# Emitting the convolutions of a hybrid decoder layer one attention half later, tied behind the score maxima

## The chip, the cores and the metric

The kernel runs on one core of one Trainium2 chip. The core has five engines that each work through their own list of instructions in order: PE (TensorE, matrix products), DVE (VectorE), ACT (ScalarE), POOL (GpSimd) and SP (SyncE, which here only issues transfers). They wait for one another through semaphores. The metric is the device time of one execution in microseconds (us); lower is better.

## The reference

One layer of a decoder that mixes sliding-window attention and a gated linear recurrence over T = 1024 tokens (plus 16 learned meta tokens in front, so 1040 rows), model width 1024, everything in float32. Cut to what matters:

```python
h = concat(meta, x)                       # 1040 x 1024
u = rmsnorm(h, g_pre_mix)
q, k, v, xr, yr = split(u @ w_in)         # widths 512, 128, 128, 512, 512
attn = sliding_window_attention(q, k, v, sinks)   # 8 heads, 2 kv heads, window 128
xr = causal_depthwise_conv(xr, conv_w, conv_b)    # 4 taps per channel
r, i = sigmoid(gate_r(xr)), sigmoid(gate_i(xr))   # block-diagonal products
a = exp(-8 * r * softplus(-lam))
hr = scan(h_t = a_t * h_(t-1) + sqrt(1 - a_t^2) * i_t * xr_t)
rec = gelu(yr) * hr
h = h + rmsnorm(concat(attn, rec) @ w_out, g_post_mix)
u = rmsnorm(h, g_pre_ffn)
h = h + rmsnorm(relu(u @ w_ff1)^2 @ w_ff2, g_post_ffn)
return h[16:]
```

A score is masked, its row maximum is taken together with the head's sink, and the exponentials are normalised by their sum plus that of the sink.

## The kernel before

**Precision.** A float32 product is made of three products of a narrower type. `split` (L94 to L100) takes a tile apart into a high part (a cast on ACT, L95, or on DVE, L97) and a low part (a subtraction on DVE, L98); `mm3` then issues three matmuls, high by high (L124), high by low (L125) and low by high (L126).

**Stages.** The normalised input `u` stays on chip in eight high and low pairs (`a` tiles). The projections come next: k, v, the first q and the first x chunk at the start, the rest during attention. Attention goes over four head pairs `j` and two halves of the tokens, eight steps in all. In each, `scores(j, half)` computes two score tiles (`bp` 0 and 1): matmuls into the bank `ps_s` (L525, L529), on DVE a fused masking and maximum (L545), on ACT the exponentials, on DVE a reciprocal (L555), on POOL the sum of the two window blocks (L559), on DVE the normalisation (L560). `attend` of the step before transposes the probabilities on PE (L571), splits them, masks them on POOL (L575), multiplies by the values (L585) and copies the result out (ACT L598, DVE L599).

**Fills.** After each `scores`, one further projection is issued to keep PE at work between the attention products: q1, x1, q2, x2, q3, x3, y0, y1 in the eight steps, y2 after the loop, and y3 after the gates. A fill loads its weight one step ahead (`load_cols`: a DMA into `raw`, then `split` into a `ws` pair), runs 24 matmuls a piece into `ps_acc` (L124 to L126, `ps_acc<-a,ws`) and evicts. For an x chunk the fill also runs the convolution `conv`: one `tensor_scalar` (L608) and three `scalar_tensor_tensor` (L613) on DVE, each over about 1040 columns. The y chunks are evicted by DVE copies (L640).

**What sets the order.** The program is written in one order, and a scheduler then orders the instructions of each engine by priority and dependencies. `deferred(FILL_LAG)` gives what is issued inside it a later priority by 1000, so that fills stand behind attention work that was issued later; steps in `Q_SLOTS` use 0. `behind(name, *instructions)` adds a dependency without a semaphore: the scheduler must place the instructions after the named one.

**After attention.** `gates(c)` for the four chunks (matmuls `ps_s`, `ps_pt`, `ps_o` `<-b,e`, each followed by a sigmoid on ACT, then `L715` on DVE), then for two pairs of chunks `decay` (an exponential and a tanh on ACT, L82 as all of its table functions) and `recur` (a square root on ACT, then on DVE L728, L729 and the scan L730). The output weights `wo[0]` to `wo[3]` are loaded and split: `wo[0]` on DVE alone (L97, then the low part L98 into `ws`), the others with their high part cast on ACT (`a<-raw`, `a<-d`). `rec_out` (gelu on ACT, L736 on DVE) gives the recurrent half of the mix. The output projection `out_mm` starts on the attention part: `ps_pt`, `ps_o`, `ps_acc`, `ps_s` `<-ws,b` and `<-a,b`. Then come the output norms (`out_norm`) and the feed-forward layer, which fill the rest of the time from about 350 us on.

Of the kernel before, what the change touches and what calls it, by code (L numbers as in the profile page):

```python
# [37 lines left out]
def hybrid_layer(  # L38
# [6 lines left out]
    nc = tc.nc  # L45
# [12 lines left out]
    def slot(tag, shape, dt=F32):  # L58
        uid[0] += 1
        return slab.tile(shape, dt, tag=tag, name=f"{tag}{uid[0]}", bufs=bufs[tag])  # L60

    def pair(tag, shape):
        return slot(tag, shape, F32R), slot(tag, shape, F32R)

    def bank(tag, shape=(P, 512)):
        uid[0] += 1
        return ps.tile(list(shape), F32, tag=tag, name=f"ps_{tag}{uid[0]}")

    def f32(ap):
        return ap.bitcast(F32)  # L70

    @contextmanager
    def deferred(n):
        tc.cur_priority += n
        yield
        tc.cur_priority -= n
# [4 lines left out]
    def lut(*args, **kwargs):  # L81
        ins = nc.scalar.activation(*args, **kwargs).ins  # L82
        if last_lut[0] is not None:
            tc.add_manual_dep(
                ins, last_lut[0],
                mybir.DependencyInfo(
                    mybir.DependencyClass.NoSync, mybir.DependencyReason.DATA
                ),
                reason="lut",
            )  # L90
        last_lut[0] = ins.name

    def split(hi, lo, src, eng=None):
        if eng is None:  # L94
            nc.scalar.copy(hi, src)  # L95
        else:
            eng.tensor_copy(hi, src)  # L97
        low = nc.vector.tensor_tensor(lo, src, f32(hi), op=ALU.subtract).ins  # L98
        mark[0] = low.name
        return low  # L100
# [4 lines left out]
    def behind(name, *inss):  # L105
        for ins in inss:
            tc.add_manual_dep(
                ins, name,
                mybir.DependencyInfo(
                    mybir.DependencyClass.NoSync, mybir.DependencyReason.DATA  # L110
                ),
                reason="order",
            )
# [60 lines left out]
    last_pow = [None]  # L174


    def load_cols(cols, tag="ws"):
        raw = slot("raw", [P, KC, P])
        o = 0
        for c0, n in cols:  # L180
            w, lo = c0
            nc.sync.dma_start(
                raw[:, :, o : o + n],
                w[:, lo : lo + n].rearrange("(k p) c -> p k c", p=P),
            )
            o += n
        hi, lo_ = pair(tag, [P, KC, P])
        split(hi, lo_, raw)
        return hi, lo_

    def w_q(j):
        return load_cols([((w_in, Q_COL + P * j), P)])

    def w_x_chunk(c):
        return load_cols([((w_in, X_COL + P * c), P)])

    def w_y_chunk(c):
        return load_cols([((w_in, Y_COL + P * c), P)])
# [19 lines left out]
    def project(w, pieces, sink):  # L218
        wh, wl = w
        for t0, n in pieces:  # L220
            acc = bank("acc")
            for kc in range(KC):
                uh, ul = u[kc]
                mm3(
                    acc[:, :n], (wh[:, kc, :], wl[:, kc, :]),
                    (uh[:, t0 : t0 + n], ul[:, t0 : t0 + n]),
                    kc == 0, kc == KC - 1,
                )
            sink(acc[:, :n], t0, n)
# [160 lines left out]
    def new_x(tag="d"):  # L390
        xr = slot(tag, [P, TT])

        def sink_x(acc, t0, n):
            nc.scalar.copy(xr[:, t0 : t0 + n], acc)

        return xr, sink_x
# [106 lines left out]
    def at_pair(cp):  # L503
        for half in range(2):
            at[half][cp] = pair("b", [P, 2, 512])


    def scores(j, half, q):

        g, pairs = j // 2, []  # L510
        for bp in range(2):
            sn = slot("c", [P, 4, 257])
            negm = small.tile([P, 4], F32, name="negm", tag="negm")
            den = small.tile([P, 4], F32, name="den", tag="den")
            rden = small.tile([P, 4], F32, name="rden", tag="rden")
            nc.vector.tensor_copy(
                sn.rearrange("p (h i) k -> p h i k", h=2)[:, :, :, 256],
                nsink[:, 2 * j : 2 * j + 2].to_broadcast([P, 2, 2]),
            )
            for h in range(2):  # L520
                sp_ = bank("s", (P, 2, 256))

                def qk(dst, b, hi, lo):
                    c = slice(b * P, (b + 1) * P)
                    nc.tensor.matmul(  # L525
                        dst, q[h][:, c], hi, start=True, stop=False,
                        skip_group_check=True,
                    )
                    nc.tensor.matmul(  # L529
                        dst, q[h][:, c], lo, start=False, stop=True,  # L530
                        skip_group_check=True,
                    )

                for i in range(2):
                    b = 4 * half + 2 * bp + i
                    if b == 0:
                        qk(sp_[:, i, 0:P], b, km[:, g, 0, :], km[:, g, 1, :])
                        qk(sp_[:, i, P:256], b, khh[g][:, 0:P], kl[g][:, 0:P])
                    else:
                        c = slice((b - 1) * P, (b + 1) * P)  # L540
                        qk(sp_[:, i, :], b, khh[g][:, c], kl[g][:, c])
                for i in range(2):
                    b = 4 * half + 2 * bp + i
                    k = 2 * h + i
                    nc.vector.tensor_tensor_reduce(  # L545
                        out=sn[:, k, 0:256], in0=sp_[:, i, :],
                        in1=mask1 if b == 0 else mask, scale=-1.0,
                        scalar=nsink[:, 2 * j + h : 2 * j + h + 1],
                        op0=ALU.add, op1=ALU.min, accum_out=negm[:, k : k + 1],
                    )  # L550
                    lut(
                        sn[:, k, :], sn[:, k, :], AF.Exp, scale=-1.0,
                        bias=negm[:, k : k + 1], accum_out=den[:, k : k + 1],
                    )
            nc.vector.reciprocal(rden, den)  # L555


            one = sn[:, :, 0:P]
            nc.gpsimd.tensor_tensor(one, one, sn[:, :, P:256], op=ALU.add)  # L559
            nc.vector.tensor_tensor(one, one, rden.to_broadcast([P, 4, P]), op=ALU.mult)  # L560
            pairs.append(sn)
        return pairs
# [40 lines left out]

    xc = [None] * NLRU

    def conv(c, xr, tag="d"):
        y = slot(tag, [P, TT])
        nc.vector.tensor_scalar(  # L608
            y, xr, prm[:, c, 3:4], prm[:, c, 4:5], op0=ALU.mult, op1=ALU.add
        )  # L610
        for k in (2, 1, 0):
            s = 3 - k
            nc.vector.scalar_tensor_tensor(  # L613
                y[:, s:], xr[:, : TT - s], prm[:, c, k : k + 1], y[:, s:],
                op0=ALU.mult, op1=ALU.add,
            )
        xc[c] = y

    ys = [None] * NLRU

    def fill_q(j):
# [3 lines left out]
            qs[j] = q  # L625
        return run

    def fill_x(c):
        def run(w):
            xr, sink = new_x()  # L630
            project(w, ALL, sink)
            conv(c, xr, "b" if c == 3 else "d")
        return run

    def fill_y(c):
# [9 lines left out]

    qs = [q0] + [None] * 3
    conv(0, xr0)
    fills = []
    for kind, j in (("q", 1), ("x", 1), ("q", 2), ("x", 2), ("q", 3), ("x", 3)):
        if kind == "q":  # L650
            fills.append((lambda j=j: w_q(j), fill_q(j)))
        else:
            fills.append((lambda j=j: w_x_chunk(j), fill_x(j)))
# [4 lines left out]
    def next_fill():  # L658
        i = len(loaded) - 1
        if i + 1 < len(fills):  # L660
            loaded.append(fills[i + 1][0]())
        else:
            loaded.append(None)
        fills[i][1](loaded[i])
# [3 lines left out]
    for j in range(NPAIR):  # L668
        for half in range(2):
            if j % 2 == 0 and half == 0:  # L670
                at_pair(j // 2)
            sn = scores(j, half, qs[j])
            with deferred(0 if (j, half) in Q_SLOTS else FILL_LAG):
                next_fill()
            if prev is not None:
                attend(*prev)
            prev = (j, half, sn)
    with deferred(FILL_LAG):
        next_fill()
    attend(*prev)  # L680
# [678 lines left out]
```

## Time and profile before

| what | value |
|---|---|
| median of 3 runs | 963.28 us (963.26 to 963.48) |
| the profiled execution's own time | 963.19 us |
| its span, first to last instruction | 960.8 us |
| mean granted clock of PE | 0.998 |
| attention (first scores L525 at 60.4 us) with fills, up to the gates | 60 to 200 us |
| gates, recurrence and the first output products, about | 200 to 270 us |

A row of the timeline has the start and the length in us, the engine, the line, the operation and `out<-in` by the names of the tiles; square brackets give the idle time before it and what ended it. A row of a chain or a group has the same names. `x2` stands for two instructions that are shown as one. A row of the waits says which engine waited for which, in us in all, how often, and the longest.

### The profile page before, as it was taken

The page shows a single profiled execution, that of the slowest core. Times are in us where ns is not written, and L with a number is a line of the kernel's source. Part 1 is how long each engine was busy: PE and PEld are TensorE (multiplying, and loading weights), DVE is VectorE, ACT ScalarE, POOL GpSimd, SP SyncE. Part 2 cuts the span into 40 slices and gives each one's busy share as a digit, 9 for nine tenths or more (in the row PEclk, how much of TensorE's full clock was granted, in tenths as well). Part 3 has the DMA queues.
Part 4 walks back from the last instruction along what each step waited for, and adds up shares of the span by engine and source line. Part 5 has one row for each costly group of instructions (what it writes and reads, how often), then busy time and mean ns, then how long its engine had stood idle before and what let it go on. Part 6 is the DMA issues. An engine that isn't in the chain of part 4 may idle for free.

```text
span 960.8 us, 12386 instructions
## 1 busy us (share of the span) xinstructions
PE 941.4 (98%) x4654; PEld 789.1 (82%) x4654; DVE 669.6 (70%) x945; ACT 501.1 (52%) x822; POOL 156.7 (16%) x202
## 2 busy tenths in 40 slices
PE   6999999999999999999999999999999999999997
PEld 6999998888788877888888888788888888888886
DVE  5579989756955796664655465568557776779884
ACT  7556676469634663443555556554433343435441
POOL 4015656600021100000111001100111100003020
PEclk9999999999999999999999999999999999999999
DMA  8111101111235457676546557623667765556422
GB/s 293 46 48 42 39 7 45 41 58 67 87 132 175 150 180 224 192 263 197 197 161 216 163 193 252 213 95 120 171 171 192 194 225 194 180 196 155 110 88 87
DMA packets 85626, 140.74 MB, mean 146 GB/s; under 512 B 5784, under 2 KB 48936, under 8 KB 85568
## 3 DMA queue, kind: packets, MB, share of 16 engines
q1 hardware_dynamic: 75104, 108.51, 34.5%
q0 software_dynamic: 9600, 29.36, 11.7%
q10 hardware_dynamic: 864, 2.10, 0.6%
q8 instruction: 36, 0.59, 0.3%
q14 instruction: 22, 0.18, 0.1%
HBM read 115.70 MB, written 23.07 MB: 144 GB/s over the span
## 4 chain that ended last, share of the span: by engine, by line
PE 88%; issue 5%; ACT 3%; DVE 2%; DMA 1%; POOL 1%; DVEq 0%; SPq 0%; POOLq 0%; ACTq 0%
PE ps_acc L124 11%; PE ps_acc L125 10%; PE ps_acc L126 10%; PE ps_s L126 6%; PE ps_s L125 6%; PE ps_s L124 6%; PE ps_pt L124 6%; PE ps_pt L125 6%; PE ps_pt L126 6%; PE ps_o L124 5%; PE ps_o L126 5%; PE ps_o L125 5%; PE ps_o L585 1%; ACT c L82 1%; PE ps_s L525 1%
## 5 line engine op out<-in xcount | busy, mean ns | idle before, releaser
L95 ACT CAST ws<-raw 128x1024 fp32r<-128x1024 f32 (+1 forms) x70 | 71.8, 1025 | 122.6 <-PE ps_o L125 45.1
L98 DVE TENSOR_TENSOR ws<-raw,ws 128x1024 fp32r<-128x1024 f32 (+1 forms) x71 | 86.3, 1215 | 47.9 <-ACT ws L95 47.8
L124 PE MATMUL ps_acc<-a,ws 128*128 128x256 f32 (+2 forms) x256 | 85.2, 333 | 0.0
L125 PE MATMUL ps_acc<-a,ws 128*128 128x256 f32 (+2 forms) x256 | 84.8, 331 | 0.0
L126 PE MATMUL ps_acc<-a,ws 128*128 128x256 f32 (+2 forms) x256 | 84.8, 332 | 0.0
L98 DVE TENSOR_TENSOR b<-b,b 128x1024 fp32r<-128x1024 f32 (+2 forms) x48 | 57.6, 1200 | 27.0 <-PE ps_o L125 17.4
L95 ACT CAST ws<-e 128x1024 fp32r<-128x1024 f32 x42 | 43.9, 1045 | 60.3 <-PE ps_o L125 26.7
L98 DVE TENSOR_TENSOR ws<-e,ws 128x1024 fp32r<-128x1024 f32 x42 | 51.3, 1222 | 23.0 <-ACT ws L95 23.0
L95 ACT CAST b<-b 128x1024 fp32r<-128x1024 f32 (+2 forms) x48 | 49.5, 1030 | 34.2 <-DVE b L862 33.4
L575 POOL TENSOR_SCALAR_AFFINE_SELECT c<-c 128x512 fp32r<-128x512 f32 x64 | 55.7, 893 | 27.3 <-ACT c L95 15.4
L169 POOL TENSOR_TENSOR rs<-ms,half_pow 128x1 f32<-128x1 f32 (+1 forms) x29 | 21.0, 730 | 211.0 <-DVE ms L165 209.6
L126 PEld LDWEIGHTS ps_acc<-a,ws 128*128 128x128 f32 x256 | 48.2, 188 | 4.9
L124 PEld LDWEIGHTS ps_acc<-a,ws 128*128 128x128 f32 x256 | 48.2, 188 | 4.2
L125 PEld LDWEIGHTS ps_acc<-a,ws 128*128 128x128 f32 x256 | 48.1, 188 | 4.2
L124 PE MATMUL ps_acc<-ws,b 128*128 128x512 f32 (+1 forms) x120 | 46.3, 386 | 0.0
L125 PE MATMUL ps_acc<-ws,b 128*128 128x512 f32 (+1 forms) x120 | 46.0, 384 | 0.0
L126 PE MATMUL ps_acc<-ws,b 128*128 128x512 f32 (+1 forms) x120 | 46.0, 384 | 0.0
L125 PE MATMUL ps_pt<-ws,b 128*128 128x512 f32 x112 | 44.2, 395 | 0.6 <-DVE ws L98 0.6
L126 PE MATMUL ps_pt<-ws,b 128*128 128x512 f32 x112 | 43.9, 392 | 0.0
L124 PE MATMUL ps_pt<-ws,b 128*128 128x512 f32 x112 | 43.9, 394 | 0.0
L124 PE MATMUL ps_s<-ws,b 128*128 128x512 f32 x110 | 43.3, 395 | 0.0
L126 PE MATMUL ps_s<-ws,b 128*128 128x512 f32 x110 | 43.2, 393 | 0.0
(393 smaller groups left out, 2713.4 us busy)
## 6 DMA issues: line engine op xcount, KB each, us to landing
raw<-in_w_ff_dram SPq DMA_DIRECT2D x58, 512.0 KB, 4.3
e<-in_w_ff_dram SPq DMA_DIRECT2D x42, 512.0 KB, 3.9
raw<-in_w_in_dram SPq DMA_DIRECT2D x12, 512.0 KB, 4.9
d<-in_w_ff_dram SPq DMA_DIRECT2D x12, 512.0 KB, 3.8
s_dram<-d POOLq DMA_DIRECT2D x12, 512.0 KB, 3.9
e<-in_w_ff_dram POOLq DMA_DIRECT2D x10, 512.0 KB, 5.4
raw<-in_w_ff_dram POOLq DMA_DIRECT2D x10, 512.0 KB, 5.6
c<-in_x_dram SPq DMA_DIRECT2D x8, 512.0 KB, 8.1
```

What stands on the lines that cost most here:

```text
L82: ins = nc.scalar.activation(*args, **kwargs).ins
L95: nc.scalar.copy(hi, src)
L98: low = nc.vector.tensor_tensor(lo, src, f32(hi), op=ALU.subtract).ins
L124: nc.tensor.matmul(dst, lh, rh, start=start, stop=False, skip_group_check=True)
L125: nc.tensor.matmul(dst, lh, rl, start=False, stop=False, skip_group_check=True)
L126: last_mm[0] = nc.tensor.matmul(dst, ll, rh, start=False, stop=stop, skip_group_check=True).ins.name
L169: last_pow[0] = nc.gpsimd.tensor_tensor(rs[:n], ms[:n], half_pow[:n], op=ALU.pow).ins.name
L525: nc.tensor.matmul(dst, q[h][:, c], hi, start=True, stop=False, skip_group_check=True,)
L575: nc.gpsimd.affine_select(out=m[:, :, side, :], in_=f32(m)[:, :, 1, :], pattern=[[0, 4], [-sign, P]], compare_op=op, fill=0.0, base=0, cha ...
L585: nc.tensor.matmul(po[:, :, oc : oc + n], v, m[:, :, pc : pc + n], start=first and k == 0, stop=last and k == 1, skip_group_check=True,)
```

## The change

Two things move, and no operation is added or taken away. The low part of each weight that `load_cols` fetches is tied behind a maximum, the last one (`h` = 1, `i` = 1) of the first score tile (`bp` = 0) of the latest `scores` issued by then. And a fill of an x chunk no longer emits its convolution: it puts it on the list `waiting`, and the loop emits it after the `scores` of the next step, outside the deferred priority, with its four instructions tied behind that step's maximum in the same way. The convolution of chunk 0, before the loop, stays as it was.

```diff
+    first_max = [None]
+
     def load_cols(cols, tag="ws"):
...
         hi, lo_ = pair(tag, [P, KC, P])
-        split(hi, lo_, raw)
+        low = split(hi, lo_, raw)
+        if first_max[0]:
+            behind(first_max[0], low)
         return hi, lo_
...
-                    nc.vector.tensor_tensor_reduce(
+                    top = nc.vector.tensor_tensor_reduce(
                         out=sn[:, k, 0:256], in0=sp_[:, i, :],
...
-                    )
+                    ).ins
+                    if bp == 0:
+                        first_max[0] = top.name
...
-    def conv(c, xr, tag="d"):
+    def conv(c, xr, tag="d", after=None):
         y = slot(tag, [P, TT])
-        nc.vector.tensor_scalar(
+        taps = [nc.vector.tensor_scalar(
...
+        if after:
+            behind(after, *taps)
...
+    waiting = []
+
     def fill_x(c):
         def run(w):
             xr, sink = new_x()
             project(w, ALL, sink)
-            conv(c, xr, "b" if c == 3 else "d")
+            waiting.append((c, xr, "b" if c == 3 else "d"))
         return run
...
             sn = scores(j, half, qs[j])
+            while waiting:
+                conv(*waiting.pop(), first_max[0])
             with deferred(0 if (j, half) in Q_SLOTS else FILL_LAG):
                 next_fill()
...
+    while waiting:
+        conv(*waiting.pop())
     with deferred(FILL_LAG):
         next_fill()
```

More of the change, by code (lines that the diff above doesn't have):

```diff
@@ L604, in hybrid_layer @@
     xc = [None] * NLRU
-    def conv(c, xr, tag="d"):
+    def conv(c, xr, tag="d", after=None):
         y = slot(tag, [P, TT])
-        nc.vector.tensor_scalar(
+        taps = [nc.vector.tensor_scalar(
             y, xr, prm[:, c, 3:4], prm[:, c, 4:5], op0=ALU.mult, op1=ALU.add
-        )
+        ).ins]
         for k in (2, 1, 0):
             s = 3 - k
-            nc.vector.scalar_tensor_tensor(
+            taps.append(nc.vector.scalar_tensor_tensor(
                 y[:, s:], xr[:, : TT - s], prm[:, c, k : k + 1], y[:, s:],
                 op0=ALU.mult, op1=ALU.add,
-            )
+            ).ins)
         xc[c] = y
+        if after:
+            behind(after, *taps)
     ys = [None] * NLRU
```

## The prediction

> **What bounds the kernel now.** I read the page's share of busy time first, then what PE waited for, then busy time by stretches of the stage that the change touches, then the chain of waits there.
>
> ```profile
> span 960.8 us, 12386 instructions
> ...
> PE 941.4 (98%) x4654; PEld 789.1 (82%) x4654; DVE 669.6 (70%) x945; ACT 501.1 (52%) x822; POOL 156.7 (16%) x202
> ...
> PEclk9999999999999999999999999999999999999999
> ...
> PE 88%; issue 5%; ACT 3%; DVE 2%; DMA 1%; POOL 1%; DVEq 0%; SPq 0%; POOLq 0%; ACTq 0%
> ```
>
> PE is busy for 941.4 of 960.8 us, at full clock, and carries 88% of the chain that ended last. Anything on another engine counts only where PE runs dry. So the question is which waits of PE the change makes, lengthens or removes. PE's own waits (columns: total, times, longest) are few:
>
> ```profile
> PE ps_s L126 <- DVE ws L98: 1.9, 2, 1.1
> PE ps_s L525 <- DVE negm L545: 1.7, 2, 1.3
> ...
> PE ps_acc L124 <- ACT a L1057: 0.7, 1, 0.7
> PE ps_pt L124 <- ACT a L95: 0.6, 1, 0.6
> PE ps_pt L125 <- DVE ws L98: 0.6, 1, 0.6
> ```
>
> The windows show in which stretch they lie (span 960.8, columns: length, then each engine's busy time, then PE clock):
>
> ```profile
> 150.00:160.00 10.00, 8.27 (x62) 7.68 (x62) 9.84 (x20) 5.99 (x16) 5.88 (x4) 1.00 0.26 76
> 160.00:200.00 40.00, 40.00 (x232) 34.93 (x231) 34.09 (x62) 22.72 (x50) 18.85 (x20) 1.00 0.16 47
> 200.00:230.00 30.00, 30.00 (x154) 26.52 (x154) 10.11 (x11) 23.16 (x36) 0.00 (x0) 1.00 0.11 36
> 230.00:250.00 20.00, 18.85 (x81) 14.72 (x80) 20.00 (x19) 19.93 (x25) 0.00 (x0) 1.00 0.23 80
> 250.00:350.00 100.00, 100.00 (x467) 82.05 (x467) 72.04 (x105) 50.80 (x111) 12.76 (x25) 1.00 0.48 158
> 940.00:960.80 20.80, 14.41 (x80) 12.29 (x78) 11.32 (x23) 4.37 (x14) 0.00 (x0) 0.89 0.26 101
> ```
>
> PE idles for 1.73 us in 150 to 160 us (10.00 less 8.27) and for 1.15 us in 230 to 250. In 160 to 230 and 250 to 350 it never idles. The remaining idle time lies at the ends or later than 350 us. The waits for `L1057` and `ps_s L126` with `ws` are outside the stretch that changes.
>
> The gap at 155 us by the chain of waits:
>
> ```profile
> 152.98 1.20 DVE d L613
> 154.18 1.57 DVE ws L98
> 155.75 0.40 DVE c L545
> ...
> 156.19 1.10 ACT c L82 x4
> ...
> 158.68 0.35 PE ps_s L525
> ```
>
> A convolution tap (`L613`) and then the low part of a fetched weight (`L98`, `ws`) stand on DVE ahead of the maxima (`L545`), so ACT's exponentials and PE's next scores (`L525`) come late. It looks like just what the change is meant for.
>
> **The change part by part.** It adds and removes no instruction: each engine has as many as before. The ties carry no semaphore, so no engine waits for anything new; they only limit the order that the scheduler may write down. What they do is therefore read from the order of the built program's instructions on each engine, set beside that of before.
>
> Ties. Nine low parts (all fetched weights but the first, which is loaded before any maximum exists) and twelve taps (three convolutions of four) are tied. Up to about 162 us of before, every engine's order is the same instruction by instruction, both convolutions there and their low parts included: the tie is to the maxima of the first score tile of that half, and these operations stood behind those already. The gap above, between the maxima of the *next* tile, keeps its cause. Cost and gain: 0.
>
> The third convolution and the low part beside it. Here order does change (half 0 and 1 of the last head pair, some 165 to 195 us): DVE gets the last score tile's normalisation (`L560`) ahead of `ws` low and the first tap instead of behind, the taps are interleaved otherwise, and PE's transposes (`L571`) and value products (`L585`) shift by a few places among the projection's matmuls.
>
> ```profile
> 174.06 1.12 DVE L608 TENSOR_SCALAR b<-d,prm 128x1040 f32<-128x1040 f32 x1
> ...
> 182.02 1.35 DVE L613 SCALAR_TENSOR_TENSOR b<-d,prm,b 128x1037 f32<-128x1037 f32 x1
> ```
>
> ```profile
> 203.44 1.08 ACT L95 CAST b<-b 128x1040 fp32r<-128x1040 f32 x1
> ```
>
> The convolution ended at 183.4 us and its result `b` is first read by ACT's cast at 203.44. Some 20 us cover it, so its move costs 0 (if the cover were gone, it would cost the delay itself). PE has no idle time from 160 to 200, and following each engine in the new order with the durations of before, I find every input of its shifted products ready 2 us or more ahead. So 0 here as well, but this is the least certain 0.
>
> What does matter is the consequence. With the last `L585` some 2.5 us earlier, eight projection matmuls (`ps_acc<-a,ws`) that stood ahead of the recurrence's gates now stand behind their start, and six of them behind all gates.
>
> ```profile
> 199.58 0.40 PE L126 MATMUL ps_acc<-a,ws 128*128 128x512 f32 x1
> 199.81 0.32 PE L124 MATMUL ps_s<-b,e 128*128 128x348 f32 x1
> ...
> 231.25 0.62 PE L124 MATMUL ps_pt<-ws,b 128*128 128x512 f32 x2
> ...
> 233.60 0.50 PE L125 MATMUL ps_pt<-ws,b 128*128 128x512 f32 x1 [0.56 <-DVE ws L98]
> ...
> 245.54 0.72 PE L124 MATMUL ps_pt<-a,b 128*128 128x512 f32 x2 [0.59 <-ACT a L95]
> ```
>
> One such matmul takes 0.23 us (199.58 to 199.81). The first gate product thus starts about 1.85 us earlier (8 x 0.23) and the last ends 6 x 0.23 = 1.38 us earlier; PE's total work is the same, so it reaches the output projection (231.25) when it did. Every ACT step that follows the gates (sigmoids, exponentials, square roots) moves by 1.38 us. The first square root, 226.56, becomes 225.18.
>
> DVE follows, and its order after that square root is another. Before:
>
> ```profile
> 227.66 1.24 DVE L728 SCALAR_TENSOR_TENSOR c<-b,c 128x1040 f32<-128x1040 f32 x1 [4.75 <-ACT c L82]
> 228.82 0.69 DVE L97 CAST ws<-raw 128x1024 fp32r<-128x1024 f32 x1
> 229.42 0.68 DVE L640 COPY d<-ps_acc 128x512 f32<-128x512 f32 x1
> 230.02 1.23 DVE L728 SCALAR_TENSOR_TENSOR c<-b,c 128x1040 f32<-128x1040 f32 x1
> 231.17 1.24 DVE L729 TENSOR_TENSOR c<-c,c 128x1040 f32<-128x1040 f32 x1
> 232.32 1.22 DVE L98 TENSOR_TENSOR ws<-raw,ws 128x1024 fp32r<-128x1024 f32 x1
> 233.46 1.22 DVE L98 TENSOR_TENSOR a<-raw,a 128x1024 fp32r<-128x1024 f32 x1
> 234.59 1.24 DVE L729 TENSOR_TENSOR c<-c,c 128x1040 f32<-128x1040 f32 x1
> 235.75 2.32 DVE L730 TENSOR_TENSOR_SCAN c<-b,c 128x1040 f32<-128x1040 f32 x1
> 237.98 0.67 DVE L640 COPY d<-ps_acc 128x512 f32<-128x512 f32 x1
> ```
>
> From the first `L728` at 227.66 to the low part of `wo[0]` (`ws`, 232.32) it was 4.66 us, with `L728`, `L97`, `L640`, `L728`, `L729` between. In the new order these stand there: `L728`, `L728`, `L729`, `L97`, `L640`, `L729`, `L730`, and only then `ws` low. By start-to-start steps: 1.15 + 1.15 + 1.15 + 0.60 + 0.60 + 1.15 (all from the rows above) + 2.23 (`L730`, 235.75 to 237.98) = 8.03 us. The start is 227.66 - 1.38 = 226.28, so `ws` low starts at 234.31 instead of 232.32: 1.99 us later. PE waits for exactly this (the row 233.60, 0.56 us, `<-DVE ws L98`). It has nothing else in its order to do, so its stop becomes 2.55 us: **+1.99**. `wo[0]`'s high part (`L97`) ends near 230.4, PE needs it at 231.25: 0. The queue behind `ws` low on DVE (`wo[1]` low, the second scan, evictions `L640`) is awaited by PE some 3 us later than it comes: 0.
>
> The other stop is at 245.54: 0.59 us for ACT's cast of `wo[3]`.
>
> ```profile
> 226.56 2.04 ACT L82 ACTIVATE c<-c 128x1040 f32<-128x1040 f32 x2
> ...
> 244.46 1.03 ACT L95 CAST a<-raw 128x1024 fp32r<-128x1024 f32 x1
> ```
>
> That cast is bound by the gelus and square roots ahead, so it comes 1.38 us earlier, at 243.08, and is done at 244.1. PE, late by 1.99 and taking it 10.16 us after its resumption in the new order, arrives at 235.59 + 10.16 = 245.75. The stop goes: **-0.59**. Next late would be `wo[3]`'s low part, near 247.5 against 251.5: covered.
>
> After 270 us PE's order is that of before. On SP, two loads of x for the output norms (`L805`) swap places with a neighbour; on POOL one mask (`L575`) does. ACT and DVE differ up to about 345 us (one early weight cast ahead of a norm). PE had no idle time in 250 to 350, and I find slack of 5 us or more: 0.
>
> Sum: +1.99 - 0.59 = +1.40 on the profiled execution. That took 963.19 us (960.8 span and 2.4 around it), 0.1 below the median of 963.28. Span 962.2, time **964.6 us**, +0.15%.
>
> Bounds: if the scan does not delay `ws` low and only the second stop goes, -0.6 gives 962.6. If the gates come no earlier, `ws` low starts 1.99 + 1.38 = 3.37 later and the second stop, which PE then meets 3.4 us later, goes too: +2.8; with 0.6 of new delay among the shifted `L585`, +3.4. I take the middle because the order of the instructions, which both ends contradict in one step each, gives it.
>
> [...] Nearest row: PE's clock is 1.00 over the stretch with the 1.73 us gap, while over the last 20.8 us, where PE is busy for only 14.41, it is 0.89. [...]
>
> **The rivals.**
> (1) Slower, 966.0: the gates do not come earlier. Place: ACT between the gates and the first square root. If a table load or a late input of the gates holds ACT so that the first `L728` starts at 227.66 as before, PE's stop is 3.93 us: +3.37 - 0.59 = +2.8. It passes the 0.2% from a first `L728` later than 226.9. For it: ACT ran these steps back to back, so a small loss early is kept. Against it: PE had no idle time from 160 to 230 us, so the gates' inputs were there before PE came to them.
> (2) Slower by the clock, 968.3: as (1), and the stop lowers PE's clock. Price by the row of the last stretch: 0.11 x 20.8 = 2.3 us on top. For it, only that row; against it, that PE did not idle that long in any row between. [...]
> (3) The change does nothing that counts, 963.2: something holds PE elsewhere ahead of `ws` low, or DVE runs ahead enough that its order there doesn't show. For it: nine tenths of the order is the same. Against it: DVE has no idle time at all in 230 to 250 (20.00 of 20.00), so work put ahead must delay.
> (4) Faster, 960.9: the 1.73 us gap closes as the change is meant to do it, and the 0.59 stop goes, with `ws` low not delayed: -2.3. Against it: the order on DVE around that gap is the same as before.
>
> **How the numbers follow.** About 0.2% (1.9 us, so 961.4 to 965.2) is what a measurement of this kernel can tell from no change. Forecast (964.6, give or take 0.5 for durations): 0.48, within. (1), and any unseen stop in the shifted products of like size: 0.27, slower. (2): 0.05, slower. (3): 0.12, within. (4): 0.05, faster; other gains: 0.03, which would need idle time that PE hardly has. Durations may carry a part of the forecast across 965.2; I move 0.03 for that. Faster 0.08, same 0.57, slower 0.35. The range reaches from 962.5, just under the lower bound, to 967.0 (the upper bound of +3.4 with some for durations); (2), (4) and half of what lies beside are left out, near 0.15.
>
> **What would show it.** Right: in the changed kernel's waits, PE `ps_pt L125 <- DVE ws L98` at about 2.5 us near 235.6; no wait of `ps_pt L124 <- ACT a L95`; the scan (`L730`) ahead of `ws` low on DVE; the first gate product near 198; the 1.7 us for `negm L545` unchanged. Wrong: a new wait of PE between 160 and 200 us, a stop near 233 that isn't longer, a window with a clock under 1.00 around 235, or any difference beyond 350 us.

## The result, and the profile after

Over eleven executions of each, the changed kernel takes 965.93 us in the median (963.45 to 969.48) against 962.91 us (961.27 to 963.48) before: the ratio is 1.0033, with a 95% interval of 1.0022 to 1.0045. It is slower, by some 3 us. The time lies inside the stated range (962.5 to 967.0) and above the single value (964.6).

The waits of PE in the changed kernel (columns: total, times, longest; later lines of the code have moved, so that L525 of before is L529, L545 is L549):

```profile
PE ps_pt L125 <- DVE ws L98: 2.5, 1, 2.5
PE ps_s L529 <- DVE negm L549: 1.7, 2, 1.3
...
PE ps_acc L124 <- ACT a L1071: 0.7, 1, 0.7
PE ps_s L126 <- DVE ws L98: 0.7, 1, 0.7
```

The stop for `ws L98` at `ps_pt` has grown from 0.6 to 2.5 us, the wait for ACT's cast (`ps_pt L124 <- ACT a L95`) is gone, and the 1.7 us for the maxima are as they were. The same windows as before:

```profile
150.00:160.00 10.00, 8.28 (x62) 7.69 (x62) 9.84 (x20) 6.02 (x16) 5.85 (x4) 1.00 0.25 74
160.00:200.00 40.00, 40.00 (x233) 34.94 (x232) 33.76 (x62) 22.77 (x50) 18.00 (x20) 1.00 0.16 47
200.00:230.00 30.00, 30.00 (x152) 26.28 (x151) 11.06 (x12) 24.42 (x37) 0.00 (x0) 1.00 0.10 36
230.00:250.00 20.00, 17.47 (x70) 13.81 (x69) 20.00 (x21) 19.36 (x24) 0.00 (x0) 0.91 0.31 97
250.00:350.00 100.00, 100.00 (x467) 82.03 (x466) 69.08 (x99) 48.64 (x107) 12.80 (x25) 1.00 0.43 144
600.00:625.00 25.00, 24.34 (x106) 19.47 (x105) 13.54 (x16) 13.85 (x14) 2.53 (x4) 1.00 0.66 216
```

From 230 to 250 us PE is busy for 17.47 us instead of 18.85, and PE's clock, 1.00 in every other row here, is 0.91. In 600 to 625 us the execution profiled before had PE idle for 1.86 us and this one for 0.66; a further execution of the same changed kernel had 1.70, so this is not of the change. It hides 1.2 us of the loss in the spans of the two profiles, 960.8 and 963.0 us.

The order of DVE that the prediction read out of the program is there (L742 is the former L728, L743 the former L729, L744 the scan):

```profile
226.51 2.39 DVE L742 SCALAR_TENSOR_TENSOR c<-b,c 128x1040 f32<-128x1040 f32 x2 [3.14 <-ACT c L82]
228.82 1.24 DVE L743 TENSOR_TENSOR c<-c,c 128x1040 f32<-128x1040 f32 x1
229.97 0.69 DVE L97 CAST ws<-raw 128x1024 fp32r<-128x1024 f32 x1
...
231.17 1.24 DVE L743 TENSOR_TENSOR c<-c,c 128x1040 f32<-128x1040 f32 x1
232.32 2.32 DVE L744 TENSOR_TENSOR_SCAN c<-b,c 128x1040 f32<-128x1040 f32 x1
234.56 1.20 DVE L98 TENSOR_TENSOR ws<-raw,ws 128x1024 fp32r<-128x1024 f32 x1
```

The scan stands ahead of the low part of `wo[0]`, which starts at 234.56 (the prediction had 234.31). And this is what PE makes of it:

```profile
232.89 0.40 PE L124 MATMUL ps_acc<-ws,b 128*128 128x512 f32 x1
235.81 0.80 PE L125 MATMUL ps_pt<-ws,b 128*128 128x512 f32 x1 [2.53 <-DVE ws L98]
236.41 0.63 PE L126 MATMUL ps_pt<-ws,b 128*128 128x512 f32 x1
236.83 0.63 PE L124 MATMUL ps_pt<-a,b 128*128 128x512 f32 x1
...
238.97 0.53 PE L126 MATMUL ps_o<-ws,b 128*128 128x512 f32 x1
239.33 0.39 PE L124 MATMUL ps_o<-a,b 128*128 128x512 f32 x1
239.56 0.39 PE L125 MATMUL ps_o<-ws,b 128*128 128x512 f32 x1
```

The row at 235.81 has the stop, 2.53 us. What follows was not in the sum: the matmuls start 0.43 us apart (236.41 to 236.83) until 239.33, and 0.23 us apart from there on. In a finer cut of the same stretch (columns as above):

```profile
234.50:235.00 0.50, 0.00 (x0) 0.00 (x0) 0.50 (x2) 0.50 (x1) 0.00 (x0) 1.00 0.00 0
...
235.50:236.00 0.50, 0.19 (x1) 0.19 (x2) 0.50 (x2) 0.50 (x1) 0.00 (x0) 0.84 0.00 0
236.00:236.50 0.50, 0.50 (x2) 0.40 (x3) 0.50 (x1) 0.50 (x2) 0.00 (x0) 0.50 0.00 0
...
238.50:239.00 0.50, 0.50 (x3) 0.36 (x2) 0.50 (x1) 0.50 (x1) 0.00 (x0) 0.50 0.97 123
239.00:239.50 0.50, 0.50 (x3) 0.46 (x2) 0.50 (x2) 0.50 (x1) 0.00 (x0) 0.74 0.61 205
239.50:240.00 0.50, 0.50 (x3) 0.40 (x3) 0.50 (x2) 0.49 (x2) 0.00 (x0) 1.00 0.83 328
```

By the means of the first and the last row under 1.00, PE ran at half clock from 235.84 to 239.26, which is 3.4 us. Eight matmuls take 3.52 us (235.81 to 239.33) where eight at the old spacing take 1.85: **1.67 us** on top of the stop.

### The profile page after: what moved, and what is told of

Same layout as the page of the kernel before. It is cut to its first block, busy times and chain, and to the rows that moved or that the text cites. A ratio compares the mean times of both kernels' runs of the same rounds, so it can differ in the third digit from the quotient of the medians.

```text
span 963.0 us, 12388 instructions
## 1 busy us (share of the span) xinstructions
PE 943.4 (98%) x4654; PEld 790.6 (82%) x4654; DVE 669.6 (70%) x945; ACT 501.2 (52%) x822; POOL 156.0 (16%) x202
## 4 chain that ended last, share of the span: by engine, by line
PE 89%; issue 4%; DVE 3%; ACT 2%; DMA 1%; POOL 1%; DVEq 0%; SPq 0%; POOLq 0%
PE ps_acc L124 11%; PE ps_acc L125 11%; PE ps_acc L126 11%; PE ps_s L126 6%; PE ps_pt L125 6%; PE ps_s L125 6%; PE ps_s L124 6%; PE ps_pt L126 6%; PE ps_pt L124 6%; PE ps_o L125 5%; PE ps_o L126 5%; PE ps_o L124 5%; PE ps_o L591 1%; ACT c L82 1%; PE ps_o L850 1%
## 5 line engine op out<-in xcount | busy, mean ns | idle before, releaser
L95 ACT CAST ws<-raw 128x1024 fp32r<-128x1024 f32 (+1 forms) x70 | 71.8, 1025 | 127.6 <-PE ps_o L125 45.3
L98 DVE TENSOR_TENSOR ws<-raw,ws 128x1024 fp32r<-128x1024 f32 (+1 forms) x71 | 86.1, 1213 | 42.3 <-ACT ws L95 42.3
L124 PE MATMUL ps_acc<-a,ws 128*128 128x256 f32 (+2 forms) x256 | 85.3, 333 | 0.0
L95 ACT CAST ws<-e 128x1024 fp32r<-128x1024 f32 x42 | 43.9, 1045 | 61.4 <-PE ps_o L125 26.8
L98 DVE TENSOR_TENSOR b<-b,b 128x1024 fp32r<-128x1024 f32 (+2 forms) x48 | 57.6, 1201 | 25.9 <-PE ps_o L125 17.4
L98 DVE TENSOR_TENSOR ws<-e,ws 128x1024 fp32r<-128x1024 f32 x42 | 51.4, 1223 | 22.8 <-ACT ws L95 22.8
L95 ACT CAST b<-b 128x1024 fp32r<-128x1024 f32 (+2 forms) x48 | 49.5, 1030 | 33.0 <-DVE b L876 32.2
L124 PEld LDWEIGHTS ps_acc<-a,ws 128*128 128x128 f32 x256 | 48.2, 188 | 4.2
L124 PE MATMUL ps_acc<-ws,b 128*128 128x512 f32 (+1 forms) x120 | 46.2, 385 | 0.0
L124 PE MATMUL ps_pt<-ws,b 128*128 128x512 f32 x112 | 43.9, 394 | 0.0
L124 PE MATMUL ps_s<-ws,b 128*128 128x512 f32 x110 | 43.3, 395 | 0.0
```

Of the source, the lines that this page charges most:

```text
L124: nc.tensor.matmul(dst, lh, rh, start=start, stop=False, skip_group_check=True)
```

## The experiments

Theory A: two terms make the loss, the longer stop for the low part of `wo[0]` and the half clock that the stop brings about. Rival B: the stop alone counts, and the low clock is a coincidence of one execution. Rival C: the loss comes from the attention work that the change shifts, and the stop is a side effect.

The order of the built programs answers one question without a run. With the tie of the fetched low parts alone, every engine's order is that of before; with the moved convolutions alone, it is that of the whole change. The low parts' tie does nothing.

**The changed kernel again** (no edit).

> The changed kernel once more, as the reference point for the runs beside it. Theory A (two terms: the scan now stands ahead of the low part of wo[0] on DVE, which makes PE stop for about 2.5 us, and a stop of that length halves PE's clock for some 3.4 us, which costs another 1.6 us): a stop of 2.5 us of PE for DVE ws L98 near 236, PE clock 0.50 from there to about 239.5, time 965 to 966. Rival B (the stop alone is the loss, the low clock seen once is a coincidence of that execution): the stop of 2.5 us again, but the clock at 1.00 behind it.

965.13 us, ratio 1.0030 [1.0017, 1.0044]. The stop was 2.5 us and the clock was 0.50 from 234.33 to 237.74: in a second profile of the program half clock again, and for 3.4 us again. B's coincidence is unlikely. But this time the low clock began 0.3 us *before* PE resumed (at 234.67), while in the first profile it began right behind the resumption (235.84, behind 235.81).

**The low part ahead of the scan.** On DVE two neighbours are swapped; nothing else differs in any engine's order.

```diff
+    load_wo(0, "raw")
+    low0 = split_wo(0, "ws", nc.vector)
     for cs in ((0, 1), (2, 3)):
...
-        nc.vector.tensor_tensor_scan(r, av[c], gi, 0.0, ...)
+        scans[c] = nc.vector.tensor_tensor_scan(r, av[c], gi, 0.0, ...).ins
+        if c == 0:
+            behind(low0.name, scans[c])
...
-    load_wo(0, "raw")
...
-    split_wo(0, "ws", nc.vector)
```

> The changed kernel with one swap: the low part of wo[0] stands directly ahead of the first scan on DVE instead of directly behind it; PE, ACT and the rest stand as in the changed kernel. Theory A: the low part starts 2.24 us earlier, PE's stop shrinks from 2.53 to about 0.3 us, the clock stays at 1.00, and PE, now some 3.9 us earlier, meets ACT's cast of wo[3] again with a stop of about 1 us: 2.9 us less than the changed kernel, within 0.2% of the kernel before. Rival B: stop of 0.3 but only about 1.2 us gained. Rival C (the loss comes from the shifted attention work, not from this stop): time stays at 965 to 966.

962.28 us, ratio 0.9995 [0.9983, 1.0007], on the same chip as the run before it. Waits of PE:

```profile
PE ps_pt L124 <- ACT a L95: 0.5, 1, 0.5
...
PE ps_pt L125 <- DVE ws L98: 0.3, 1, 0.3
```

The window from 230 to 250 us has PE busy for 19.20 us and a clock of 1.00. One swap takes back 2.85 us, as much as A's expectation said (2.9), while the attention part stays that of the changed kernel. C, in the form that all the loss comes from there, is out. By the stops alone (2.53 to 0.31, and 0.49 at the cast) B would give 1.73 us; with the clock A gives 3.4. The intervals leave about 1.7 us either way on the measured 2.85, so the times lean to A without deciding; what decides is the clock of 1.00 in the profile.

**A stop in between.** The first scan is cut in two and the low part of `wo[0]` stands between the pieces; x is 780 in one kernel and 520 in the other.

```diff
-        nc.vector.tensor_tensor_scan(r, av[c], gi, 0.0, ...)
+        first = nc.vector.tensor_tensor_scan(r[:, :x], av[c][:, :x], gi[:, :x], 0.0, ...).ins
+        load_wo(0, "raw")
+        low = split_wo(0, "ws", nc.vector)
+        behind(first.name, low)
+        rest = nc.vector.tensor_tensor_scan(r[:, x:], av[c][:, x:], gi[:, x:], r[:, x-1:x], ...).ins
+        behind(low.name, rest)
```

> The changed kernel with the first scan cut in two at column 780 of 1040; the low part of wo[0] stands between the pieces. PE's stop should be 0.3 + 780/1040 of 2.24 = 2.0 us. Theory A in its loose form (a stop of 2 us already counts as idle): clock 0.50 for some 3.4 us behind it, time 0.5 us under the changed kernel. Theory A in a strict form (it takes more than 2 us): clock 1.00, time 2.2 us under the changed kernel.

> As the run before with the cut at column 520: a stop of 0.3 + 1.12 = 1.4 us, little more than the 1.26 us of the gap at 158 us behind which the clock stayed at 1.00. Theory A: no lower clock, time 2.5 us or so under the changed kernel, and a stop of 0.3 us or less at the cast of wo[3]. If the clock falls here too, the gap at 158 us was spared for another reason than its length.

Cut at 780: 965.31 us, ratio 1.0031 [1.0019, 1.0044]. Cut at 520: 964.16 us, 1.0016 [1.0006, 1.0026]. PE with the cut at 780:

```profile
233.15 0.40 PE L124 MATMUL ps_acc<-ws,b 128*128 128x512 f32 x1
235.54 0.50 PE L125 MATMUL ps_pt<-ws,b 128*128 128x512 f32 x1 [1.99 <-DVE ws L98]
...
236.80 0.39 PE L124 MATMUL ps_pt<-a,b 128*128 128x512 f32 x1
237.03 0.58 PE L125 MATMUL ps_o<-ws,b 128*128 128x512 f32 x1
237.41 0.63 PE L126 MATMUL ps_o<-ws,b 128*128 128x512 f32 x1
...
239.97 0.63 PE L126 MATMUL ps_acc<-ws,b 128*128 128x512 f32 x1
240.40 0.45 PE L124 MATMUL ps_acc<-a,b 128*128 128x512 f32 x1
240.68 0.40 PE L125 MATMUL ps_s<-ws,b 128*128 128x512 f32 x1
```

A stop of 1.99 us is enough. But the spacing changes only at 237.03, 1.5 us after PE resumed, and goes back at 240.40: again 3.4 us. With the cut at 520 the stop was 1.45 us, and the window from 230 to 250 us has a clock of 1.00. So the fall does not go by the stop's end: it came 0.03 us behind it, 0.34 ahead of it and 1.5 behind it in three profiles, and in this one not at all.

The clock records have one length in common, 3.413 us. With the cut at 780 the clock is 0.50 from 158.57 to 161.99 and from 237.08 to 240.49 us, and the 75.09 us between the two pieces are 22 such steps. In the first profile of the changed kernel the record has 221.87 us of full clock ahead of its piece and 720.21 us from there (239.26) to the next fall, at 959.47: 65 and 211 steps. In the profile of before it has one stretch of full clock, 942.08 us: 276 steps. The pieces of half clock ahead of the kernel's end (six, in five of the fourteen profiles) are 3.4 us each, one step. Points a whole number of steps from a fall are called raster lines here. Against PE's resumption they shift from execution to execution: a line lies 0.03 us behind it in the first profile of the changed kernel and 0.34 us ahead of it in the second. Two steps ahead of a fall, each with the step behind it, in the profile of the cut at 780 (columns as above):

```profile
155.16:158.57 3.41, 1.70 (x12) 1.55 (x13) 3.32 (x11) 3.34 (x11) 1.27 (x1) 1.00 0.52 154
158.57:161.99 3.42, 3.42 (x18) 3.42 (x17) 3.29 (x13) 2.62 (x9) 1.22 (x1) 0.50 0.03 5
...
233.67:237.08 3.41, 1.54 (x7) 1.28 (x8) 3.41 (x4) 3.38 (x4) 0.00 (x0) 1.00 0.17 38
237.08:240.49 3.41, 3.41 (x10) 2.63 (x9) 3.41 (x4) 3.38 (x4) 0.00 (x0) 0.50 0.78 269
```

PE is idle for about half of the step ahead of either fall: 1.71 us in the first, 1.87 in the second. The first is the gap before the maxima's scores, which left the clock at 1.00 in the profile of before; there a raster line at 157.62 divides the gap into 0.67 and 1.06 us. Ahead of the changed kernel's fall at 235.84 it was 2.53 us in the step, ahead of the one at 234.33 in its second profile 2.19, and ahead of the falls at the kernel's end 2.82 (changed, first profile) and 1.92 us (before). From the first clock record on (14.0 and 14.3 us) the other steps at full clock of these last two profiles have 1.27 and 1.15 us at most, with no fall behind them. There was none behind the stop of 1.45 us with the cut at 520 either, nor behind one step with 1.89 us, in the next experiment.

Neither time came out as A had it. The cut at 780 was to be 0.5 us under the changed kernel and is 0.2 us over it, with a second piece of half clock in its profile. The cut at 520 was to be some 2.5 us under it and is 1.0 us under. It is 1.2 us slower than its terms beside the swap (+1.14 for the stop, -0.49 for the cast, measured +1.9). Its one profile, of the second fastest of its twelve executions (962.13 us), shows no reason, and the two intervals leave 1.5 us either way; this stays open.

**The kernel before with the low part pushed back**, nothing of the change in it:

```diff
-    split_wo(0, "ws", nc.vector)
+    behind(prods[1].name, split_wo(0, "ws", nc.vector))
```

where `prods[1]` is the second L729.

> The kernel before, with nothing of the change, but the low part of wo[0] tied behind the second product L729 of the recurrence, which puts that product and the low part of wo[1] ahead of it on DVE (1.13 + 1.16 = 2.3 us). Theory A: PE's stop grows from 0.56 to 2.85 us, the clock halves for some 3.4 us, the stop of 0.59 us at the cast of wo[3] goes: +2.3 + 1.6 - 0.6 = +3.3 us, about 966, although convolutions and attention are as before. Rival C (the loss of the changed kernel comes from its attention work): +2.3 at most from the stop, clock at 1.00.

965.89 us, ratio 1.0034 [1.0023, 1.0045]: the whole loss, without the change. The profiled execution of it is a surprise:

```profile
PE ps_pt L125 <- DVE ws L98: 2.8, 1, 2.8
```

```profile
230.00:250.00 20.00, 17.15 (x74) 13.63 (x73) 20.00 (x19) 19.62 (x25) 0.00 (x0) 1.00 0.27 86
```

A stop of 2.8 us and a clock of 1.00. The mean granted clock of each execution tells that the profiled one was not the usual case. Eight of the ten had 0.995 or 0.996, with 964.9 to 967.8 us; the other two, the profiled one among them, had 0.998 and 0.999, with 963.6 and 962.2. Of the 32 executions of the kernel before beside them, five had 0.996 and none less. By the mean clocks, a lower clock came with the longer stop in eight executions of ten.

In this profile a raster line at 234.17 divides the stop into 1.89 and 0.96 us:

```profile
230.76:234.17 3.41, 1.52 (x7) 0.90 (x5) 3.41 (x4) 3.41 (x4) 0.00 (x0) 1.00 0.13 29
```

With the line inside the stop the clock stayed at 1.00 here, as it did with the divided gap in the profile of before. But 1.89 us is a little more than the 1.71 and 1.87 us behind which the clock fell with the cut at 780, so idle time alone doesn't tell the two apart, and what does stays open.

**Both causes repaired, with the change and without it.** Beside the low part of `wo[0]`, tied ahead of both products L729 and the scan, ACT's cast of `wo[3]` is tied ahead of the first gelu. On the changed kernel and on the kernel before alike:

```diff
+    load_wo(0, "raw")
+    low0 = split_wo(0, "ws", nc.vector)
     for cs in ((0, 1), (2, 3)):
...
+        if c == 0:
+            behind(low0.name, prods[c])
+        if c == 1:
+            behind(low0.name, prods[c])
+        if c == 0:
+            behind(low0.name, scans[c])
...
-        lut(y, y, AF.Gelu_apprx_tanh)
+        ins = lut(y, y, AF.Gelu_apprx_tanh)
+        if c == 0 and half == 0:
+            behind(highs[3], ins)
```

> The changed kernel with both causes taken away: the low part of wo[0] ahead of both products L729 and the first scan, and ACT's cast of wo[3] ahead of the first gelu. Theory A: no stop of PE in 230 to 250 us, clock 1.00, 1.15 us less than the kernel before (0.56 + 0.59), so ratio 0.9988. Rival C: the shifted attention work costs something of its own, and it stays level with the kernel before or over it.

> The kernel before with the same two repairs and without the change. Theory A: both stops gone, 1.15 us less than the kernel before, level with the changed kernel so repaired: the change by itself is worth nothing on either side once the recurrence's order is set by hand. Rival C: faster than the changed kernel so repaired.

> The kernel before with both repairs of the recurrence once more, as the reference point of the run beside it: no stop of PE from 230 to 250 us, 1.15 us under the kernel before by the terms, ratio about 0.9988.

> The changed kernel with both repairs once more, beside the kernel before with the same repairs, since the first pair (0.9997 and 0.9987) left open whether the change costs anything of its own. Theory A: no cost of its own beside a chance that the 1.73 us gap before 158 us halves the clock in some executions, which both kernels have; ratio within 0.0007 of the other's. Rival C: 0.7 us or more over the other again.

> The kernel before with both repairs a third time: 0.997 to 0.999 of the kernel before, after 0.9987 and 0.9972. By the terms of the profile (0.56 + 0.59 us) it is 0.9988.

With the change: 962.61 us, 0.9997 [0.9988, 1.0006], and 963.16 us, 0.9993 [0.9980, 1.0007]. Without it: 961.89 us, 0.9987 [0.9978, 0.9997]; 960.92 us, 0.9972 [0.9962, 0.9982]; 961.42 us, 0.9980 [0.9969, 0.9991]. All three are faster than the kernel before, and the kernel before so repaired is the fastest here; the terms (0.56 + 0.59 us, 0.9988) lie within two of the three intervals. From 230 to 250 us neither has a stop of PE left; the first row is that of the repaired kernel before, the second that of the repaired changed kernel:

```profile
230.00:250.00 20.00, 20.00 (x88) 16.21 (x87) 20.00 (x19) 19.93 (x25) 0.00 (x0) 1.00 0.32 107
```

```profile
230.00:250.00 20.00, 20.00 (x88) 16.18 (x88) 20.00 (x20) 19.89 (x25) 0.00 (x0) 1.00 0.32 107
```

With the repairs the changed kernel stayed 0.7 and 1.7 us behind the kernel before with them, by the medians of either pair on one chip. The intervals of each pair overlap. But both pairs point the same way, and in the second the ratios are 0.0013 apart, where A had 0.0007 at most and rival C 0.7 us or more. So A's "worth nothing on either side" is doubtful, and a cost of the change's own of some 1 us is likelier; where it arises is not shown. Seven of the 23 repaired executions with the change had a mean clock of 0.996, and none of the 34 without it. The two profiles of the former have waits of 0.5 and 1.5 us for a `ws` low part in 625 to 930 us, where the order of all engines is the same in both kernels; the three profiles of the latter have none. Over all profiles, PE was idle for 0.4 to 1.6 us in that stretch in six of the eight with the change, and for 0.2 us in one of the six without it. Why these weights come late there was not tried.

The first of these profiles with the change shows the half clock at the same place as the first piece with the cut at 780 (timeline, then two steps of the raster, columns as above):

```profile
156.01 0.36 PE L530 MATMUL ps_s<-b,b 128*128 128x256 f32 x1 [0.47 <-DVE negm L550]
...
157.98 0.36 PE L530 MATMUL ps_s<-b,b 128*128 128x256 f32 x1 [1.26 <-DVE negm L550]
```

```profile
155.19:158.61 3.42, 1.69 (x12) 1.33 (x12) 3.33 (x13) 3.04 (x10) 1.27 (x1) 1.00 0.54 153
158.61:162.02 3.41, 3.41 (x18) 3.41 (x17) 3.31 (x12) 2.93 (x10) 0.85 (x1) 0.50 0.02 5
```

The two stops of 0.47 and 1.26 us before the maxima's scores, which both kernels have always had, fell into one step of the raster here: 1.73 us.

**Two tries at that gap.** One ties everything that the change ties to the maxima of the *second* score tile (`if bp == 1` in place of `if bp == 0`), with both repairs; the other leaves the change out and ties one low part alone, with both repairs:

```diff
             sn = scores(j, half, qs[j])
+            if (j, half) == (3, 0):
+                behind(second_max[0], fetched[5])
```

Here `second_max[0]` is the last maximum of the second score tile and `fetched[5]` the low part of the third x chunk's weight.

> As the changed kernel with both repairs, and the ties to the maxima of the second score tile of the half instead of the first. The gap of PE before 159 us came from a convolution tap and a low part on DVE ahead of the second tile's maxima, so both now stand behind them. Theory A: the waits for negm L545 go from 1.7 us to 0.5 or less, 1.2 to 1.7 us less than with the repairs alone, ratio to before 0.997. Rival: low parts that come later make the fills wait instead (a new wait for ws L98 between 60 and 200 us), and the gain is eaten.

> The kernel before with both repairs, and one fetched low part (the sixth, that of the third x chunk, which stood on DVE between the last tap and the maxima at 154.2 us) tied behind the maxima of the second score tile of half (3, 0). Theory: the 1.73 us gap of PE before 159 us goes for the most part, and with it the chance that an idle window there halves the clock: 1.0 to 2.5 us under the repairs alone. Rival: PE's order changes with it, and the weight now comes late for its own fill, with a new wait for ws L98 or a bank between 150 and 200 us: level or slower than the repairs alone.

The first: 964.72 us, 1.0020 [1.0010, 1.0030]. The wait for the maxima is gone, and there is another:

```profile
89.43 0.35 PE L125 MATMUL ps_acc<-a,ws 128*128 128x256 f32 x1 [1.56 <-DVE b L118]
```

It comes with 1.1 us more for an eviction on ACT (`ps_acc <- ACT d`), and 0.5 us for `ws` low is back in 230 to 250 us. The rival's mechanism holds in kind, by a bank that is evicted late and not by a weight. The second: 962.11 us, 0.9982 [0.9971, 0.9993], 1.2 us over the repairs alone beside it (960.92). The scheduler rearranged PE as well, and the two stops became a single one of 1.62 us, behind which the profile has half clock from 155.4 to 158.8. Neither is better than the repairs.

## Why the prediction was right or wrong

- *The ties cost and gain nothing up to 162 us.* Right: the waits for the maxima are 1.7 us before and after, and windows 150 to 160 and 160 to 200 show the same busy time.
- *No new wait of PE among the shifted products of attention.* Right: 40.00 of 40.00 us in 160 to 200.
- *The gates start 1.85 us earlier and end 1.38 us earlier.* The first gate product is at 198.11 instead of 199.81, 1.70 earlier. ACT's first square root is at 225.40 instead of 226.56, 1.16 earlier. PE in this execution was 0.25 us later anyway (231.50 against 231.25), which makes it 1.4 and more.
- *The low part of `wo[0]` 1.99 us later, PE's stop 2.55 us.* Measured 2.53. Right, and the swap shows that it is this and not the attention work.
- *The stop of 0.59 us at the cast goes.* Right: no such wait in the changed kernel.
- *The step that failed:* the sum has no term for PE's clock, which puts it at 0 for the stop of 2.55 us; the prediction held the fall of the clock for a matter of the slower rival alone, with a stop of 3.9 us. No run shows that 0, and no row of before showed that a stop of 2.55 us is too short. The runs showed 1.67 us behind the stop of 2.53 us, and half clock behind steps of 3.413 us in which PE was idle for 1.71 to 2.53 us.
- *The row that was weighed against a lower clock* was the gap of 1.73 us with the clock at 1.00. It proved less than it seemed to: a raster line divided the gap in that execution (0.67 and 1.06 us), and half clock stood behind the same gap in two later profiles, where it lay in one step (1.71 us with the cut at 780, 1.73 with both repairs).

The trace of before already had a case against the clock term of 0, in the last stretch, from which the prediction took only a price. PE's last matmul ended at 954.42 us, and the clock fell at 956.34, with 1.92 us of idle time in the step ahead:

```profile
952.92:956.34 3.42, 1.50 (x13) 1.29 (x11) 2.93 (x8) 1.31 (x5) 0.00 (x0) 1.00 0.64 246
956.34:959.75 3.41, 0.00 (x0) 0.00 (x0) 1.42 (x2) 0.00 (x0) 0.00 (x0) 0.50 0.40 154
```

Without the low clock the forecast held, as far as few executions can tell: of the changed kernel's eighteen in its two runs, three had a mean clock of 0.998 or 0.999, and these took 964.39, 964.72 and 964.72 us, beside 964.6.

With the term put right the sum is +1.97 - 0.59 + 1.67 = +3.05 us, against +3.0 in the medians (2.1 to 4.3 by the interval). So the likeliest case (within 0.2%, with 0.48) had the mechanism and not the size, and the outcome was that of the rivals with 0.35: slower, at about the price of rival (1), by the mechanism of rival (2), at the stop of the forecast. That the time fell on rival (1)'s 966.0 is luck: its stop of 3.93 us didn't come, and the half clock made up for what was missing.

## What to carry to other kernels

Count a stop of PE twice: its length, and what a lower clock can take behind it, which here was 1.67 us behind the stop of 2.53 us and nothing in the profile with 1.45. Two short stops close together can count as well: half clock stood behind 0.47 and 1.26 us in one profile with both repairs, and not behind the same two in the profile of before. A tie that fixes the order in one stage can loosen it in the next: the scheduler's order of a stage that nobody touched has to be read again, and where a neighbour's place is worth 2 us, it is worth a tie of its own.

## What the runs showed of the hardware

Half clock (0.50, with matmuls 0.43 us apart instead of 0.23) came in pieces of 3.41 us: 235.84 to 239.26 and 234.33 to 237.74 in the first and second profile of the changed kernel, 237.08 to 240.49 with the cut at 780. They did not all begin with PE's own resumption, which was 0.03 us ahead of the first, 0.34 behind the start of the second and 1.54 ahead of the third. The 75.09 us between the two pieces with the cut at 780 are 22 times 3.413 us, and the full clock of 720.21 us in the changed kernel and of 942.08 us in the kernel before are 211 and 276 times.

The steps of 3.413 us ahead of a fall had PE idle for 1.71 and 1.87 us (cut at 780), 1.73 (both repairs, with the change), 1.92 (before, at the end), and 2.53, 2.19 and 2.82 us (changed kernel, the last at the end). No fall stood behind steps with up to 1.27 us (changed) and 1.15 us (before), behind the stop of 1.45 us with the cut at 520, or behind one step with 1.89 us (kernel before with the low part pushed back). These are single profiles, and the idle time was not swept.

Executions of one program differed: with the stop of 2.85 us the profiled one had 1.00 from 230 to 250 us and a mean of 0.998, while eight of ten had means of 0.995 or 0.996; with the gap of 1.73 us the clock fell to 0.50 in the first profile of the repaired changed kernel and stayed at 1.00 in the second. The mean granted clock was 0.995 to 0.997 in the five profiles with a piece of half clock ahead of the end and 0.998 or 0.999 in the nine without; it does not say behind which stop.
